# Five of sixteen row-tile pairs of the MLP's second product by Strassen's form: seven block products instead of eight

## Chip, cores and metric

One core of one Trainium2 chip runs the whole kernel as one launch. The metric is the device time of an execution in microseconds. Before the change it is 1999.34 us, the median of 3 runs (1997.73 to 1999.47).

The engines are called as in the profile: PE multiplies matrices (PEld loads its stationary operand), DVE is VectorE, ACT is ScalarE, POOL is GpSimd, SP issues most of the DMAs. Results of PE land in PSUM, which has eight accumulator banks of 128 x 512 float32.

## What is computed

The input is 256 tokens of width 2048. Two layers follow, the first with a convolution module as its mixer, the second with latent attention (MLA). After each mixer stands a squared-ReLU MLP of width 8192, all in float32:

```python
def sq_relu_mlp(h, w1, w2):
    return jnp.square(jax.nn.relu(h @ w1)) @ w2
...
    for layer in range(DEPTH):
        ...
        h = rms_norm(x, norm_mlp_g[layer])
        x = x + sq_relu_mlp(h, mlp_w1[layer], mlp_w2[layer])
    return rms_norm(x, final_norm_g)
```

The change concerns the product with `w2`, an 8192 x 2048 matrix, in both layers.

## The kernel before

**Numbers in two parts.** Each float32 operand of a product is split into a rounded part `hi` and the remainder `lo`, both of type float32r. A product is then three matmuls into the same bank: hi·hi, lo·hi, hi·lo (`mm3`, L182 to L186). Weights are loaded in units of 1 MB (`load`, L143, three `raw` buffers, issued by SP), and each unit is split in two halves (`split_half`, L152): ACT copies `raw` to `hi` (L158), DVE subtracts `hi` from `raw` (L159). `hi` and `lo` have six buffers each (`WB`, L42), each of 128 x 1024; a half takes one of each. So at most three units are split or being used at once.

**The MLP** (`mlp`, L383) works in two halves of the inner width (`HALVES`), each with 32 of the 64 row tiles of `w2`, and each in two stages:

- The first product runs in eight groups of four column tiles (L392). Weights are stationary, activations `xt` move: L403 multiplies by the 512 columns that hold both parts of 256 tokens, L404 by 256. After each group, L408 to L416 sum the parts, square the positive values and split them into `gh` and `gl`, one 128 x 256 block for each row tile of `w2`.
- The second product (`product_A`, L343) runs over four column blocks `n` of 512 columns. For each block, two PSUM banks (one for each token tile `t` of 128) collect 32 row tiles `k`: activations are stationary (`gh`, `gl`), weights of 128 x 512 move. The loop over units of four row tiles loads and splits one unit, then issues 4 x 2 x 3 matmuls. At the block's end `add` (L322, L327) adds the two banks, scaled by the token's factor `r2`, to the residual `xs`.

In the second half of each layer, finished columns of `xs` are prepared for the next stage (`prepare`, L332): transposed on PE (`to_T`, L235, L240) into PSUM banks of the kind `tr` and split into `xt`, and squared and summed on ACT (L339). One column block is prepared while the next is multiplied. In the last layer nothing is transposed; the final norm (`finish`, L1348) works on the token tiles one after the other, each after its last matmuls: the last column block holds back three units and multiplies them for `t` = 0, then for `t` = 1, so that the end of `t` = 0 lies beside the matmuls of `t` = 1. `before` (L1376) multiplies the first three column blocks by the gain ahead of that.

**PSUM.** From the convolution's second product on, the eight banks are split into six of kind `acc` and two of kind `tr` (L760).

**Order.** Outside of blocks marked `manual_schedule` (most of the two mixers) a scheduler sets each engine's order when the kernel is built: of the instructions that are ready by its own reckoning it takes the earliest in the program. Each engine then works through its list strictly in that order on the chip. A buffer is given to a new tile when its old tile has been read for the last time. The MLP lies outside of the marked blocks.

Of the kernel before, what the change touches and what calls it, by code (L numbers as in the profile page):

```python
# [10 lines left out]
F32 = mybir.dt.float32  # L11
F32R = mybir.dt.float32r
# [3 lines left out]
ALU = mybir.AluOpType  # L16
# [60 lines left out]
def trunk_kernel(  # L77
# [66 lines left out]

# [172 lines left out]
    def residual_stage(last, gain, r_scale=None):  # L317


        ssq = small.tile([P, T, NNB], F32, tag="ssq", name=nm("ssq")) if last else None  # L320

        def add(n, ps, t):  # L322
            sl = slice(n * NB, (n + 1) * NB)
            if r_scale is None:
                nc.vector.tensor_tensor(xs[:, t, sl], ps[t], xs[:, t, sl], op=ALU.add)
            else:
                nc.vector.scalar_tensor_tensor(  # L327
                    out=xs[:, t, sl], in0=ps[t], scalar=r_scale[:, t : t + 1], in1=xs[:, t, sl],
                    op0=ALU.mult, op1=ALU.add,
                )  # L330
# [49 lines left out]
        while due:  # L380
            prepare(due.pop(0))

    def mlp(layer, ssq, next_gain, finish=None, before=None):  # L383

        with ExitStack() as cx:
            mp = cx.enter_context(tc.tile_pool(name=f"mp{layer}", bufs=1, reuse_waits="tile"))
            nkh = FF // P // HALVES
            r2 = small.tile([P, T], F32, tag="r2", name=nm("r2"))
            nssq = None
            for hf in range(HALVES):  # L390
                hh, hl = [], []
                for g in range(nkh // 4):  # L392
                    ps = [acc_tile() for _ in range(4)]
                    c0 = (hf * nkh + 4 * g) * P
                    for u in range(KC // 4):
                        wj = load_split([rows(mlp_w1[layer], 4 * u, 4, c0, NB)], 4)
                        for j in range(4):
                            k = 4 * u + j
                            wh, wl = wj(j)
                            for b in range(4):  # L400
                                bs = slice(b * P, (b + 1) * P)

                                nc.tensor.matmul(ps[b], wh[:, bs], xhl(k), start=k == 0, stop=False)  # L403
                                nc.tensor.matmul(ps[b][:, :S], wl[:, bs], xh(k), start=False, stop=k == KC - 1)  # L404
                    gh = mp.tile([P, 4, S], F32R, tag="gh", name=nm("gh"), bufs=nkh // 4)
                    gl = mp.tile([P, 4, S], F32R, tag="gl", name=nm("gl"), bufs=nkh // 4)
                    for b2 in range(2):
                        v = mp.tile([P, 2, S], F32, tag="v", name=nm("v"), bufs=2)  # L408
# [4 lines left out]
                        nc.vector.scalar_tensor_tensor(out=v, in0=v, scalar=0.0, in1=v, op0=ALU.max, op1=ALU.mult)  # L413
                        bs = slice(2 * b2, 2 * b2 + 2)
                        nc.scalar.activation(gh[:, bs, :], v, AF.Copy)
                        nc.vector.tensor_tensor(gl[:, bs, :], v, gh[:, bs, :].bitcast(F32), op=ALU.subtract)  # L416
                    hh.append(gh)
                    hl.append(gl)
# [3 lines left out]
                nssq, add, prepare = residual_stage(hf == HALVES - 1, next_gain, r2)  # L422
                product_A(
                    mlp_w2[layer],
                    hf * nkh,
                    nkh,
                    lambda k, t: hh[k // 4][:, k % 4, t * P : (t + 1) * P],
                    lambda k, t: hl[k // 4][:, k % 4, t * P : (t + 1) * P],
                    add,
                    prepare,  # L430
                    finish=(lambda t: finish(nssq, t)) if finish is not None and hf == HALVES - 1 else None,
                    before=lambda: before(nssq),
                )
            return nssq


    with ExitStack() as cx:
# [218 lines left out]
        with tc.manual_schedule():  # L656
# [680 lines left out]
        product_A(mla_w_o[0], 0, H, oh_kt, ol_kt, add, prepare, range(2, NNB), range(2))  # L1337


    with tc.tile_pool(name="fin", bufs=1, reuse_waits="tile") as fp:  # L1340
        gf = fp.tile([P, D], F32, name="gf")
        nc.scalar.dma_start(gf, final_norm_g.rearrange("(a n) -> a n", a=1).partition_broadcast(P))

        def gained(t, n):
            sl = slice(n * NB, (n + 1) * NB)
            nc.vector.tensor_tensor(xs[:, t, sl], xs[:, t, sl], gf[:, sl], op=ALU.mult)

        def finish(ssq, t):  # L1348

            n = NNB - 1  # L1350
            sl = slice(n * NB, (n + 1) * NB)
            v = small.tile([P, 1], F32, tag="msf", name=nm("ms"))
            w = small.tile([P, 1], F32, tag="wsf", name=nm("ws"))
            y = small.tile([P, 1], F32, tag="ysf", name=nm("ys"))
            q = small.tile([P, 1], F32, tag="qsf", name=nm("qs"))
            nc.vector.tensor_scalar(v, ssq[:, t, n : n + 1], scalar1=1.0 / D, scalar2=part[t], op0=ALU.mult, op1=ALU.add)
            nc.scalar.activation(w, v, AF.Sqrt)
            nc.vector.reciprocal(y, w)
            nc.vector.scalar_tensor_tensor(out=q, in0=y, scalar=v, in1=y, op0=ALU.mult, op1=ALU.mult)
            nc.vector.tensor_scalar(q, q, scalar1=-0.5, scalar2=1.5, op0=ALU.mult, op1=ALU.add)  # L1360
            nc.vector.tensor_tensor(y, y, q, op=ALU.mult)
            for n in range(NNB):
                ob = xs[:, t, n * NB : (n + 1) * NB]
                if n == NNB - 1:
                    nc.vector.scalar_tensor_tensor(
                        out=ob, in0=ob, scalar=y, in1=gf[:, n * NB : (n + 1) * NB], op0=ALU.mult, op1=ALU.mult
                    )
                elif n:
                    nc.scalar.activation(ob, ob, AF.Copy, scale=y)
                else:  # L1370
                    nc.vector.tensor_scalar(ob, ob, scalar1=y, scalar2=None, op0=ALU.mult)
                nc.sync.dma_start(out[0, t * P : (t + 1) * P, n * NB : (n + 1) * NB], ob)

        part = []

        def before(ssq):  # L1376

            for t in range(T):
                m = small.tile([P, 1], F32, tag="msp", name=nm("msp"))
                nc.vector.tensor_reduce(m, ssq[:, t, : NNB - 1], axis=AX.X, op=ALU.add)  # L1380
                nc.vector.tensor_scalar(m, m, scalar1=1.0 / D, scalar2=EPS, op0=ALU.mult, op1=ALU.add)
                part.append(m)
                for n in range(NNB - 1):
                    gained(t, n)

        mlp(1, ssq, None, finish, before)


_INS = [
# [23 lines left out]
```

## Time and profile before

| | |
|---|---|
| median of 3 runs | 1999.34 us |
| profiled execution, first to last instruction (span) | 1996.1 us |
| median of the runs minus this span | 3.2 us |
| PE busy | 1971.3 us (99%) |
| DVE busy | 1212.9 us (61%) |
| ACT busy | 975.3 us (49%) |
| POOL busy | 223.8 us (11%) |
| first MLP product, first half of layer 0 | 316.4 to 494.9 us |
| second MLP product, first half of layer 0 | 494.9 to 669.0 us |

The profile is one execution, with times from the first instruction. The span leaves out what lies before the first and after the last instruction; the runs' times hold it. A matmul's row gives its duration from its start to its modelled end, and the next matmul starts before that end, so the time that a matmul costs is read from the distance between starts.

### The profile page before, as it was taken

What the parts mean: (1) busy time and instruction counts of PE and PEld (TensorE: products, weight loads), DVE (VectorE), ACT (ScalarE), POOL (GpSimd) and SP (SyncE); (2) the same over time, 40 slices, a digit from 0 to 9 for tenths busy, and PEclk for the clock granted to TensorE, in tenths of its full rate; (3) what the DMA queues carried; (4) which work ended last, traced back from release to release, by engine and by line L of the source; (5) the groups of instructions that cost most, each with busy time, mean ns of one, the idle gap of its engine ahead of it and who ended that gap; (6) DMA issues with size and microseconds to landing.
All of it is one profiled execution on the core that took longest, in us unless ns stands there. A gap on an engine that the chain in (4) does not pass through costs nothing.

```text
span 1996.1 us, 27859 instructions
## 1 busy us (share of the span) xinstructions
PE 1971.3 (99%) x11060; PEld 1728.7 (87%) x11060; DVE 1212.9 (61%) x1795; ACT 975.3 (49%) x1385; POOL 223.8 (11%) x184
## 2 busy tenths in 40 slices
PE   7999999999999999999999999999999999999998
PEld 7999888888888888888899998888888888888886
DVE  5999867556544555655556665656654545665553
ACT  5456655445333444544456665545443334454443
POOL 5999200000000000000001310000000000000000
PEclk9999999999999999999999999999999999999999
DMA  7666365665655666655555445666555566665553
GB/s 239 185 182 184 131 197 182 190 190 189 196 197 195 190 190 190 190 190 190 190 159 176 120 148 181 199 190 190 190 190 191 195 195 189 190 191 195 194 190 105
DMA packets 243265, 367.57 MB, mean 184 GB/s; under 512 B 15416, under 2 KB 89792, under 8 KB 242880
## 3 DMA queue, kind: packets, MB, share of 16 engines
q1 hardware_dynamic: 242112, 363.63, 57.8%
q10 hardware_dynamic: 1024, 2.17, 0.3%
q8 instruction: 86, 1.41, 0.3%
q14 instruction: 43, 0.35, 0.0%
HBM read 363.68 MB, written 2.10 MB: 183 GB/s over the span
## 4 chain that ended last, share of the span: by engine, by line
PE 90%; DVE 8%; ACT 1%; DMA 0%; issue 0%; POOL 0%; SPq 0%; ACTq 0%; DVEq 0%
PE acc L403 23%; PE acc L184 16%; PE acc L186 16%; PE acc L185 16%; PE acc L404 12%; DVE sum L591 6%; PE acc L490 1%; PE acc L489 1%; PE acc L491 1%; PE tr L240 1%; PE sum L539 0%; DMA xs<-in_x 0%; PE acc L1187 0%; ACT hi L158 0%; PE acc L1051 0%
## 5 line engine op out<-in xcount | busy, mean ns | idle before, releaser
L159 DVE TENSOR_TENSOR lo<-raw,hi 128x1024 fp32r<-128x1024 f32 (+2 forms) x630 | 760.7, 1210 | 694.3 <-ACT hi L158 682.6
L158 ACT ACTIVATE hi<-raw 128x1024 fp32r<-128x1024 f32 (+1 forms) x696 | 723.2, 1046 | 786.4 <-PE acc L185 450.3
L403 PE MATMUL acc<-xt,hi 128*128 128x512 f32 x2048 | 710.6, 390 | 0.0
L404 PE MATMUL acc<-xt,lo 128*128 128x256 f32 x2048 | 577.7, 282 | 0.0
L403 PEld LDWEIGHTS acc<-xt,hi 128*128 128x128 f32 x2048 | 384.5, 188 | 80.5
L184 PE MATMUL acc<-hi,gh 128*128 128x512 f32 x1024 | 398.6, 389 | 0.0
L186 PE MATMUL acc<-lo,gh 128*128 128x512 f32 x1024 | 398.4, 389 | 0.0
L185 PE MATMUL acc<-hi,gl 128*128 128x512 f32 x1024 | 398.4, 389 | 0.0
L404 PEld LDWEIGHTS acc<-xt,lo 128*128 128x128 f32 x2048 | 387.1, 189 | 0.1
L186 PEld LDWEIGHTS acc<-lo,gh 128*128 128x128 f32 x1024 | 192.2, 188 | 40.3
L184 PEld LDWEIGHTS acc<-hi,gh 128*128 128x128 f32 x1024 | 192.2, 188 | 39.6
L185 PEld LDWEIGHTS acc<-hi,gl 128*128 128x128 f32 x1024 | 192.2, 188 | 39.5
L591 DVE SCALAR_TENSOR_TENSOR sum<-ub,w_dw,sum 128x256 f32<-128x256 f32 x400 | 162.9, 484 | 7.1 <-ACT sum L547 6.0
L159 POOL TENSOR_TENSOR lo<-raw,hi 128x1024 fp32r<-128x1024 f32 x66 | 157.6, 2410 | 24.0 <-ACT hi L158 24.0
L489 PE MATMUL acc<-xt,hi 128*128 128x256 f32 x512 | 144.4, 282 | 0.0
L491 PE MATMUL acc<-xt,lo 128*128 128x256 f32 x512 | 143.1, 279 | 0.3 <-POOL lo L159 0.3
L490 PE MATMUL acc<-xt,hi 128*128 128x256 f32 x512 | 143.1, 279 | 0.1
L491 PEld LDWEIGHTS acc<-xt,lo 128*128 128x128 f32 x512 | 96.2, 188 | 0.5 <-POOL lo L159 0.5
L490 PEld LDWEIGHTS acc<-xt,hi 128*128 128x128 f32 x512 | 96.3, 188 | 0.3 <-DVE xt L197 0.3
L489 PEld LDWEIGHTS acc<-xt,hi 128*128 128x128 f32 x512 | 96.3, 188 | 0.0
L982 POOL MEMSET pad_kv<- 128x8 f32 x1 | 0.1, 104 | 770.0 <-PE acc L186 770.0
L411 ACT ACTIVATE v<-acc 128x256 f32<-128x256 f32 x128 | 46.4, 382 | 25.4 <-PE acc L404 25.4
(241 smaller groups left out, 1783.6 us busy)
## 6 DMA issues: line engine op xcount, KB each, us to landing
raw<-in_mlp_w SPq DMA_DIRECT2D x256, 1024.0 KB, 5.2
raw<-in_conv_w_pw SPq DMA_DIRECT2D x64, 512.0 KB, 5.2
raw<-in_conv_w_pw SPq DMA_DIRECT2D x16, 1024.0 KB, 5.1
raw<-in_mla_w_o SPq DMA_DIRECT2D x16, 1024.0 KB, 5.4
raw<-in_mla_w_kv_up SPq DMA_DIRECT2D x8, 1024.0 KB, 5.9
raw<-in_mla_w_in SPq DMA_DIRECT2D x8, 576.0 KB, 3.8
raw<-in_mla_w_in SPq DMA_DIRECT2D x4, 1024.0 KB, 5.4
raw<-in_mla_w_q_up SPq DMA_DIRECT2D x16, 256.0 KB, 3.8
```

Source lines behind the costliest of these rows:

```text
L158: nc.scalar.activation(hi, raw[:, js, :], AF.Copy)
L159: eng.tensor_tensor(lo, raw[:, js, :], hi.bitcast(F32), op=ALU.subtract)
L184: nc.tensor.matmul(ps, sh, mh, start=start, stop=False)
L185: nc.tensor.matmul(ps, sl, mh, start=False, stop=False)
L186: nc.tensor.matmul(ps, sh, ml, start=False, stop=stop)
L403: nc.tensor.matmul(ps[b], wh[:, bs], xhl(k), start=k == 0, stop=False)
L404: nc.tensor.matmul(ps[b][:, :S], wl[:, bs], xh(k), start=False, stop=k == KC - 1)
L411: nc.scalar.activation(v[:, b, :], o[:, S:], AF.Copy)
L489: nc.tensor.matmul(o, wh[:, bs], xh(k), start=k == 0, stop=False)
L490: nc.tensor.matmul(o, wh[:, bs], xl(k), start=False, stop=False)
L491: nc.tensor.matmul(o, wl[:, bs], xh(k), start=False, stop=k == KC - 1)
L591: nc.vector.scalar_tensor_tensor(out=out, in0=ubs[c][:, w : w + S], scalar=tap(c, w), in1=pcs[c], op0=ALU.mult, op1=ALU.add)
```

## The change

The 32 row tiles of a half become 16 pairs, and the four column blocks become two pairs `na`, `nb`. The unit of weights is now two row tiles by 1024 columns instead of four by 512, still 1 MB. For one such unit, two token tiles, two row tiles and two column blocks make a product of 2 x 2 blocks by 2 x 2 blocks. A plain pair does it in eight block products, as before. The pairs 0, 3, 6, 9 and 12 (`seven`) do it in seven, in Winograd's variant of Strassen's form: the activations' blocks are combined beforehand into seven operands (POOL, at the end of the first product), the weights' blocks are summed on DVE into four tiles `tt` before they are split, and the products are collected in seven banks, `P1`, `Q5`, `Q7`, `Q6`, `P4`, `P2`, `Q3`. With `Q0`, which takes the plain products that have no other bank, all eight are in use. After pair 12 the four banks P1, Q5, Q6 and Q7 are combined and added to `xs` (`early`), and become free. The other four take the plain products of three of the four output blocks (`outs`) beside their own, and are added at the end.

All eight banks are now of kind `acc`, and transposes take theirs from the same eight. `prepare` runs behind pairs 13 and 14 of the second pair of columns for the first two column blocks, and at the end for the other two. The last column pair of the last layer holds back pairs 13 to 15 and multiplies them by token tile; two column blocks instead of one are left for `finish`. The final gain is loaded at the start of the last second product instead of ahead of the MLP.

```diff
+        psum.clear()
...
     def tr_tile():
-        return psum["tr"].tile([P, NB], F32, tag="tr", name=nm("tr"))
+        return psum["tr"].tile([P, NB], F32, tag="tr", name=nm("tr")) if "tr" in psum else acc_tile()
...
+    def split_part(src, eng):
+        _, nj, cols = src.shape
+        hi = wpool.tile([P, nj, cols], F32R, tag="hi", name=nm("hi"), bufs=WB)
+        lo = wpool.tile([P, nj, cols], F32R, tag="lo", name=nm("lo"), bufs=WB)
+        nc.scalar.activation(hi, src, AF.Copy)
+        eng.tensor_tensor(lo, src, hi.bitcast(F32), op=ALU.subtract)
+        return hi, lo
+
+    NPAIR = FF // P // HALVES // 2
+    seven = lambda p: p % 3 == 0 and p < NPAIR - 1
+    LAST_SEVEN = max(p for p in range(NPAIR) if seven(p))
+    A11, A22, A12, S3, S1, S2, S4 = range(7)
+
+    def down(w, k_lo, hs, xs_add, prepare, pre, mp, finish=None, before=None):
+        for n2 in range(NNB // 2):
+            na, nb = 2 * n2, 2 * n2 + 1
+            banks, seen = {}, set()
+            outs = {(1, nb): "P2", (1, na): "Q3", (0, nb): "P4", (0, na): "Q0"}
+            def mm(name, sh, sl, mh, ml, stop):
+                if name not in banks:
+                    banks[name] = acc_tile()
+                mm3(banks[name], sh, sl, mh, ml, name not in seen, stop)
+                seen.add(name)
+            def plain(p, parts, n, t):
+                for k in range(2):
+                    wh, wl = parts[k]
+                    gh, gl = (a[:, k, t * P : (t + 1) * P] for a in hs[p])
+                    bs = slice((n - na) * NB, (n - na + 1) * NB)
+                    mm(outs[t, n], gh, gl, wh[:, 0, bs], wl[:, 0, bs], p == NPAIR - 1 and k == 1)
+            def early():
+                s1, s5 = (mp.tile([P, NB], F32, tag="v", name=nm("v"), bufs=2) for _ in range(2))
+                uv = mp.tile([P, 2, NB], F32, tag="W", name=nm("W"), bufs=1)
+                u, v = uv[:, 0, :], uv[:, 1, :]
+                nc.scalar.activation(s1, banks["P1"], AF.Copy)
+                nc.scalar.activation(s5, banks["Q5"], AF.Copy)
+                nc.vector.tensor_tensor(u, s1, banks["Q6"], op=ALU.subtract)
+                nc.vector.tensor_tensor(v, u, banks["Q7"], op=ALU.subtract)
+                xs_add(nb, s1, 1)
+                xs_add(nb, v, 0)
+                nc.gpsimd.tensor_tensor(u, s5, u, op=ALU.subtract)
+                nc.gpsimd.tensor_tensor(v, s5, v, op=ALU.subtract)
+                xs_add(na, u, 1)
+                xs_add(na, v, 0)
+            last = finish is not None and n2 == NNB // 2 - 1
+            kept = []
+            for p in range(NPAIR):
+                raw = load([rows(w, k_lo + 2 * p, 2, na * NB, 2 * NB)], 2)
+                if seven(p):
+                    x = raw.rearrange("p j (b n) -> p (j b) n", b=2)
+                    tt = mp.tile([P, 4, NB], F32, tag="T", name=nm("T"), bufs=1)
+                    nc.vector.tensor_tensor(
+                        tt[:, 0:2, :], x[:, 0:1, :].broadcast_to([P, 2, NB]), x[:, 1:3, :], op=ALU.add
+                    )
+                    one = split_part(x[:, 1:2, :], nc.vector)
+                    nc.vector.tensor_tensor(tt[:, 2, :], tt[:, 0, :], x[:, 2, :], op=ALU.add)
+                    t13 = split_part(tt[:, 0:2, :], nc.vector)
+                    nc.vector.tensor_tensor(tt[:, 3, :], tt[:, 2, :], x[:, 3, :], op=ALU.add)
+                    t24 = split_part(tt[:, 2:4, :], nc.vector)
+                    two = split_part(x[:, 2:4, :], nc.vector)
+                    gh, gl = hs[p]
+                    for name, f, part, i in (
+                        ("P1", A11, one, 0), ("Q5", S1, t13, 0), ("Q7", S3, t13, 1), ("Q6", S2, t24, 0),
+                        ("P4", A22, t24, 1), ("P2", A12, two, 1), ("Q3", S4, two, 0),
+                    ):
+                        mm(name, gh[:, f, :], gl[:, f, :], part[0][:, i, :], part[1][:, i, :],
+                           p == LAST_SEVEN and name in ("P1", "Q5", "Q6", "Q7"))
+                    if p == LAST_SEVEN:
+                        early()
+                else:
+                    parts = [split_half(raw, h, nc.vector) for h in range(2)]
+                    if last and p > LAST_SEVEN:
+                        kept.append((p, parts))
+                    else:
+                        for t in range(T):
+                            for n in (na, nb):
+                                plain(p, parts, n, t)
+                    if p > LAST_SEVEN and pre:
+                        prepare(pre.pop(0))
+            if last:
+                before()
+                for t in range(T):
+                    for n in (nb, na):
+                        for p, parts in kept:
+                            plain(p, parts, n, t)
+                        xs_add(n, banks[outs[t, n]], t)
+                        prepare(n, t)
+                    finish(t)
+            else:
+                for t, n in ((0, nb), (1, nb), (1, na), (0, na)):
+                    xs_add(n, banks[outs[t, n]], t)
+                pre += [na, nb]
...
+                        if seven(p):
+                            f = mp.tile([P, 8, P], F32, tag="W", name=nm("W"), bufs=1)
...
+                            nc.gpsimd.tensor_tensor(
+                                f[:, 4:6, :], f[:, 0:1, :].broadcast_to([P, 2, P]), f[:, 1:3, :], op=ALU.subtract
+                            )
+                            nc.gpsimd.tensor_tensor(f[:, 6, :], f[:, 1, :], f[:, 5, :], op=ALU.subtract)
+                            nc.gpsimd.tensor_tensor(f[:, 7, :], f[:, 3, :], f[:, 6, :], op=ALU.subtract)
+                            src, shape, tag = f[:, 1:8, :], [P, 7, P], "s"
...
+                        nc.scalar.activation(gh, src, AF.Copy)
+                        nc.vector.tensor_tensor(gl, src, gh.bitcast(F32), op=ALU.subtract)
+                        hs.append((gh, gl))
...
-            repool("m", acc=6, tr=2)
+            repool("m", acc=8)
...
         for n in range(NNB):
             ob = xs[:, t, n * NB : (n + 1) * NB]
-            if n == NNB - 1:
+            if n >= NNB // 2:
                 nc.vector.scalar_tensor_tensor(
...
                 )
-            elif n:
-                nc.scalar.activation(ob, ob, AF.Copy, scale=y)
             else:
-                nc.vector.tensor_scalar(ob, ob, scalar1=y, scalar2=None, op0=ALU.mult)
+                nc.scalar.activation(ob, ob, AF.Copy, scale=y)
```

More of the change, by code (lines that the diff above doesn't have):

```diff
@@ L381, in product_A @@
             prepare(due.pop(0))
-    def mlp(layer, ssq, next_gain, finish=None, before=None):
+    def split_part(src, eng):
[7 more added lines that the diff above has]
+    seven = lambda p: p % 3 == 0 and p < NPAIR - 1
@@ new lines, in trunk_kernel @@
+    LAST_SEVEN = max(p for p in range(NPAIR) if seven(p))
[78 more added lines that the diff above has]
+                pre += [na, nb]
+        if finish is None:
+            while pre:
+                prepare(pre.pop(0))
@@ L385, in mlp @@
+    def mlp(layer, ssq, next_gain, finish=None, before=None, last_w1=None):
         with ExitStack() as cx:
@@ L404, in mlp @@
                                 nc.tensor.matmul(ps[b][:, :S], wl[:, bs], xh(k), start=False, stop=k == KC - 1)
-                    gh = mp.tile([P, 4, S], F32R, tag="gh", name=nm("gh"), bufs=nkh // 4)
-                    gl = mp.tile([P, 4, S], F32R, tag="gl", name=nm("gl"), bufs=nkh // 4)
                     for b2 in range(2):
+                        p = 2 * g + b2
                         v = mp.tile([P, 2, S], F32, tag="v", name=nm("v"), bufs=2)
@@ L421, in mlp, with xs_add @@
                     nc.vector.tensor_tensor(r2, r, r, op=ALU.mult)
[L422 to L430, printed above, removed]
+                if hf == HALVES - 1 and last_w1 is not None:
+                    last_w1()
+                nssq, _, prepare = residual_stage(hf == HALVES - 1, next_gain, r2)
+                def xs_add(n, src, t):
+                    sl = slice(n * NB, (n + 1) * NB)
+                    nc.vector.scalar_tensor_tensor(
+                        out=xs[:, t, sl], in0=src, scalar=r2[:, t : t + 1], in1=xs[:, t, sl], op0=ALU.mult, op1=ALU.add
+                    )
+                down(
+                    mlp_w2[layer], hf * nkh, hs, xs_add, prepare if hf == HALVES - 1 else lambda *a: None, [], mp,
                     finish=(lambda t: finish(nssq, t)) if finish is not None and hf == HALVES - 1 else None,
@@ L1337, in trunk_kernel, with load_gain @@
         product_A(mla_w_o[0], 0, H, oh_kt, ol_kt, add, prepare, range(2, NNB), range(2))
-    with tc.tile_pool(name="fin", bufs=1, reuse_waits="tile") as fp:
-        gf = fp.tile([P, D], F32, name="gf")
+    fin = {}
+    def load_gain():
+        fp = right_pool("fin", 1)
+        fin["g"] = gf = fp.tile([P, D], F32, name="gf")
         nc.scalar.dma_start(gf, final_norm_g.rearrange("(a n) -> a n", a=1).partition_broadcast(P))
[L1344 to L1363, printed above, removed]
-                if n == NNB - 1:
-                    nc.vector.scalar_tensor_tensor(
-                        out=ob, in0=ob, scalar=y, in1=gf[:, n * NB : (n + 1) * NB], op0=ALU.mult, op1=ALU.mult
-                    )
-                elif n:
-                    nc.scalar.activation(ob, ob, AF.Copy, scale=y)
[L1370 to L1386, printed above, removed]
@@ L1389, with before @@
+    part = []
+    def before(ssq):
+        for t in range(T):
+            m = small.tile([P, 1], F32, tag="msp", name=nm("msp"))
+            nc.vector.tensor_reduce(m, ssq[:, t, : NNB // 2], axis=AX.X, op=ALU.add)
+            nc.vector.tensor_scalar(m, m, scalar1=1.0 / D, scalar2=EPS, op0=ALU.mult, op1=ALU.add)
+            part.append(m)
+            for n in range(NNB // 2):
+                gained(t, n)
+    mlp(1, ssq, None, finish, before, load_gain)
 _INS = [
```

46 lines of the change are left out of this document (39 added, 7 removed).

## The prediction

> **What bounds the kernel now.** I read the page's busy line, its clock row and its chain first, then PE's waits.
>
> ```profile
> span 1996.1 us, 27859 instructions
> ...
> PE 1971.3 (99%) x11060; PEld 1728.7 (87%) x11060; DVE 1212.9 (61%) x1795; ACT 975.3 (49%) x1385; POOL 223.8 (11%) x184
> ...
> PEclk9999999999999999999999999999999999999999
> ...
> PE 90%; DVE 8%; ACT 1%; DMA 0%; issue 0%; POOL 0%; SPq 0%; ACTq 0%; DVEq 0%
> ```
>
> ```profile
> PE tr L280 <- DMA stage<-in_conv_w_dw: 11.7, 1, 11.7
> PE sum L539 <- DVE ub L514: 2.1, 1, 2.1
> PE tr L1178 <- DVE pr L1172: 1.2, 2, 0.9
> ```
>
> PE is busy for 99% of the span at full clock, the chain that ends last is PE's for 90%, and the three longest waits of PE stand at the start, in the convolution and in the MLA; none is in the MLP. So a matmul taken out of the MLP shortens the span by what it costs PE, as long as nothing else becomes late. What it costs is not the duration of its row. Below are a group by shape, and the first and last rows of the timeline of PE over the second product of layer 0's first half (columns: start, duration, engine, line).
>
> ```profile
> L184 PE MATMUL acc<-hi,gh 128*128 128x512 f32 x1024 | 398.6, 389 | 0.0
> ```
>
> ```profile
> 494.91 0.39 PE L184 MATMUL acc<-hi,gh 128*128 128x512 f32 x1
> 495.14 0.40 PE L185 MATMUL acc<-hi,gl 128*128 128x512 f32 x1
> ...
> 668.78 0.39 PE L186 MATMUL acc<-lo,gh 128*128 128x512 f32 x1
> 669.01 0.40 PE L403 MATMUL acc<-xt,hi 128*128 128x512 f32 x1
> ```
>
> 32 row tiles x 4 blocks x 2 token tiles x 3 matmuls are 768 starts in 669.01 - 494.91 = 174.10 us: **226.7 ns** apart, while each row lasts 389 ns, since a matmul starts before the last one's modelled end. I take 226.7 ns.
>
> **What the change removes.** A seven-pair issues 7 x 3 = 21 matmuls where eight products take 24. There are 5 such pairs x 2 column pairs x 2 halves x 2 layers = 40, so 120 matmuls go: 120 x 0.2267 = **27.2 us**. A plain pair takes PE 24 x 0.2267 = 5.44 us, a seven-pair 4.76 us.
>
> The Trainium skill ("TensorE: Matmul & The Clock Gate", Back-to-back issue gap) gives a warm gap of N/2.4 + 2.5 ns, an estimate of 215.8 ns for N = 512 and of 25.9 us for the change. The trace's 226.7 ns is longer and decides.
>
> **What it adds on DVE, ACT and POOL.** The durations come from the groups by shape:
>
> ```profile
> L159 DVE TENSOR_TENSOR lo<-raw,hi 128x1024 fp32r<-128x1024 f32 x606 | 742.4, 1228 | 675.9 <-ACT hi L158 664.3 <-PE tr L240 9.6
> L158 ACT ACTIVATE hi<-raw 128x1024 fp32r<-128x1024 f32 x672 | 707.3, 1060 | 769.9 <-PE acc L185 433.7 <-PE acc L403 301.7 <-ACT gh L415 27.2
> L159 POOL TENSOR_TENSOR lo<-raw,hi 128x1024 fp32r<-128x1024 f32 x66 | 157.6, 2410 | 24.0 <-ACT hi L158 24.0
> ...
> L416 DVE TENSOR_TENSOR gl<-v,gh 128x512 fp32r<-128x512 f32 x64 | 43.8, 684 | 0.0
> L415 ACT ACTIVATE gh<-v 128x512 fp32r<-128x512 f32 x64 | 40.5, 633 | 6.3 <-DVE v L413 6.3
> ...
> L327 DVE SCALAR_TENSOR_TENSOR xs<-acc,r,xs 128x512 f32<-128x512 f32 x32 | 23.0, 751 | 11.0 <-PE acc L186 11.0
> ...
> L567 POOL TENSOR_TENSOR tp<-tp,tp 128x256 f32<-128x256 f32 x23 | 16.9, 742 | 0.2
> ...
> L325 DVE TENSOR_TENSOR xs<-acc,xs 128x512 f32<-128x512 f32 x16 | 10.6, 687 | 3.0 <-PE acc L186 3.0
> ...
> L1269 ACT ACTIVATE cq<-acc,y 128x512 f32<-128x512 f32 x2 | 1.4, 690 | 0.5 <-PE acc L186 0.5
> ```
>
> *A seven-pair.* DVE: the four sums (1.23 + 2 x 0.68 = 2.60 us), the split of `one` (0.68) and of three tiles of 1024 columns (3 x 1.23): 6.96 us, against 2.46 for a plain pair. ACT: 0.63 + 3 x 1.06 = 3.81 us against 2.12. So DVE needs more time for a seven-pair (6.96) than PE (4.76). Over three pairs, seven and plain and plain, it is 6.96 + 2 x 2.46 = 11.9 us beside PE's 4.76 + 2 x 5.44 = 15.64 us, 76%. The load fits; whether it comes in time hangs on the buffers.
>
> *`early`*, 8 times: on ACT two copies from PSUM (2 x 0.69), on DVE two differences (2 x 0.69) and four additions to `xs` (4 x 0.75), 4.4 us; on POOL two differences of 512 columns, half of 2.41 us each, 1.2 us (estimate). The four additions at the end of a column pair are as many as before.
>
> *Operands of the seven*, 20 times, on POOL: one operation of 256 columns (0.74 us) and two of 128. These lie in the first product, and pairs 0 to 12 are not multiplied until that is over.
>
> POOL and DVE hold each other up. Rows of both timelines in the MLA:
>
> ```profile
> 1108.16 0.47 POOL L898 TENSOR_TENSOR m<-scratch,cos 128x128 f32<-128x128 f32 x1
> 1108.58 1.45 POOL L899 TENSOR_TENSOR m<-scratch,sin 128x128 f32<-128x128 f32 x1
> ```
>
> ```profile
> 1108.16 1.55 DVE L159 TENSOR_TENSOR lo<-raw,hi 128x1024 fp32r<-128x1024 f32 x1 [2.20 <-ACT hi L158]
> ```
>
> The same POOL operation lasts 0.47 or 1.45 us, the second beside a DVE split, which itself lasts 1.55 instead of 1.23. So I allow the longer of the two for each POOL step on a chain: `early` takes 4.4 + 2 x 1.2 + 2 waits of about 0.75, some 8 us from its first step.
>
> In all DVE gains 40 x 4.5 + 8 x 4.4 + some 8 for wider operand splits, about 223 us (to 1436, 73% of the span), ACT about 85.
>
> **Do the weights come in time?** Today ACT waits for a buffer, not for data:
>
> ```profile
> 503.11 1.06 ACT L158 ACTIVATE hi<-raw 128x1024 fp32r<-128x1024 f32 x1 [1.65 <-PE acc L185]
> ```
>
> ```profile
> raw<-in_mlp_w SPq DMA_DIRECT2D x256, 1024.0 KB, 5.2
> ```
>
> The idle time ahead of a split ends when PE gives `hi` back; a load lands 5.2 us after its issue. I follow the six `hi`/`lo` buffers through three pairs, counted from a seven-pair's first matmul. It frees its four tiles after 3, 9, 15 and 21 matmuls: 0.68, 2.04, 3.40, 4.76 us. The plain pairs free theirs at 9.52, 10.20 and 14.96, 15.64. Each new tile takes the buffer of the tile six before it. The next seven-pair's tiles get theirs at 3.40, 4.76, 9.52 and 10.20; with 1.06 of ACT and 1.23 of DVE, and a neighbour queued ahead, its last is ready by about 13.7 and is needed at 15.64 + 15 x 0.2267 = 19.04. Its other tiles have 5 us or more. The plain pair after it gets buffers at 14.96 and 15.64, is ready by about 18.5 and is needed at 20.40. The last plain pair has 5 us. Loads: the `raw` of a seven-pair is free at about 13, lands 5.2 us later and isn't split before 19. So no step of the cycle is late; the margin is 2 to 5 us.
>
> **Seams**, where the margin is thinner:
>
> *First to second product* (4 times). In the same place today DVE does the sums of the last group and then the split of the last buffer to come free:
>
> ```profile
> 498.94 1.22 DVE L159 TENSOR_TENSOR lo<-raw,hi 128x1024 fp32r<-128x1024 f32 x1
> ```
>
> It ends 5.25 us after the second product's first matmul (494.91). In the changed kernel that is the `lo` of pair 1's second half, needed after 4.76 + 5 x 0.2267 = 5.9 us. A margin of 0.65 us; I take a loss of 0.2 each, 0 to 1.
>
> *Column pair to column pair* (4 times, and 4 ends of a half). Four banks are free since `early`; P4's is needed after 12 matmuls, 2.72 us, the others 0.68 us apart, and four additions of 0.75 us free them at that pace from 0.75 us on. Cover: 2 us, unless DVE puts two splits ahead. I take 0.15 each, 0 to 3.
>
> *End of layer 0.* 16 transposes instead of 8 follow the last matmul and wait for four additions. Today such transposes lie among the next stage's matmuls:
>
> ```profile
> 1024.32 0.30 PE L186 MATMUL acc<-lo,xt 128*128 128x288 f32 x1
> 1024.46 0.82 PE L240 MATMUL tr<-ident,xs 128*128 128x128 f32 x6
> 1025.03 0.38 PE L184 MATMUL acc<-hi,xt 128*128 128x288 f32 x1
> ```
>
> The MLA's first row tiles are ready by then, so they can go first: 0 to 3 us, I take 0.3.
>
> *The end.* Pairs 13 to 15 are held back and are read within 18 matmuls. Pair 15 gets the last buffers of pair 12 at its end, and `early` and `before` (4 x 0.68 us) compete for DVE: 0 to 3 us, I take 1. Behind the last matmul:
>
> ```profile
> 1987.29 0.75 DVE L327 SCALAR_TENSOR_TENSOR xs<-acc,r,xs 128x512 f32<-128x512 f32 x1 [4.14 <-PE acc L186]
> ...
> 1990.20 0.48 DVE L1371 TENSOR_SCALAR xs<-xs,ys 128x512 f32<-128x512 f32 x1
> 1990.61 0.74 DVE L1365 SCALAR_TENSOR_TENSOR xs<-xs,ys,gf 128x512 f32<-128x512 f32 x1
> ```
>
> DVE scales two blocks by the longer form, 0.27 us more. The gain's 1 MB load moves beside the second product, where loads wait for buffers anyway: nothing, or one load of 5.2 us late.
>
> The losses sum to 4 x 0.2 + 4 x 0.15 + 0.3 + 1 + 0.3 = 3.0 us. The sum is -27.2 + 3.0 = **-24.2 us**: a span of 1971.9 from 1996.1, and as the median of the runs lies 3.2 us above the span, **1975.1 us** from 1999.34.
>
> **Rivals.**
>
> *No bank to change to.* With all eight banks collecting, PE stands while four sums leave PSUM. If four additions (3.0 us) lay on the path at each of the 8 ends, 24 of the 27.2 us would be lost: about 1996; with half of them, 1984. For it: DVE is the busier engine, and a split ahead of an addition costs 1.23 us. Against it: `early` empties four banks ahead of the end. The Trainium skill ("Perfetto Trace Analysis", Matmuls) says that independent groups should rotate through banks, so that the evacuation of one lies beside the matmuls of the next. This change leaves only `early`'s four for that; no row of before shows all eight in use.
>
> *DVE in the wrong order* (slower). Each engine's list is fixed at build time. If a sum of the next seven-pair, waiting for its load, stands ahead of splits that PE needs, look-ahead is lost there, and PE waits for what DVE needs over PE's time (6.96 - 4.76 = 2.2 us) and for the first `hi` and `lo` (1.3 us), 3.5 us. It decides from 27.2 / 3.5 = 8 of the 40 seven-pairs. At 16 it gives 2028, at all 40 some 2112. For it: only six buffers, four to a seven-pair. Against it: the margins above, and that today's order keeps PE without a wait in the MLP.
>
> *No change*: both in part, 1995.3 to 2003.3. *More than forecast*: if a matmul cost its 389 ns, 46.7 us would go, 1953; the 768 starts speak against it. That the change doesn't remove its matmuls is excluded by the count.
>
> **How the numbers follow.** Forecast (1970 to 1979) 0.58; the banks or a few late splits take part of the gain (1979 to 1995.3) 0.20; no change 0.05; slower 0.14 (2003 to 2050 mostly); more 0.03. A measurement of this kernel can tell about 0.2%, 4 us, from no change: faster 0.81, same 0.05, slower 0.14. A range of 1970 to 1998 takes in the first two cases and part of the third, about 0.8.
>
> **What would show it.** Right: L184 to L186 have 120 fewer matmuls of 512 columns on the MLP's tiles, with starts 0.227 us apart; a second product of one half takes (768 - 30) x 0.2267 = 167.3 us instead of 174.1; DVE about 1436 us. Wrong: a wait of PE for `hi` or `lo` in each seven-pair (order), or for `xs` (banks); or starts that lie further apart.

## The result and the profile after

The changed kernel takes **1974.44 us** (median of 4 runs, 1974.37 to 1974.63), beside 1998.61 for the kernel before in the same measurements. The ratio is 0.988, with a 95% interval of 0.987 to 0.990. The forecast was 1975.1 us, with a loss of 3.0 against the 27.2 us of the removed matmuls. The measured loss is about as large, and lies at another place. Single executions of the kernel before lie near 1997.8 or near 1999.4 us, so its median depends on how many of each were taken. The profiled executions, 1996.1 and 1972.6 us from the first to the last instruction, differ by 23.5 us, a loss of 3.7.

The page of the changed kernel: span, busy times, and the clock by slices.

```profile
span 1972.6 us, 28263 instructions
...
PE 1945.4 (99%) x10940; PEld 1708.3 (87%) x10940; DVE 1410.4 (71%) x2043; ACT 1032.7 (52%) x1481; POOL 311.0 (16%) x260
...
PEclk9999999999999999999999999999999999999999
```

PE has 120 matmuls fewer, and is still busy for 99%. DVE was busy for 197.5 us more, where 223 were forecast. PE's waits:

```profile
PE tr L281 <- DMA stage<-in_conv_b_dw: 11.6, 1, 11.6
PE sum L669 <- DVE ub L644: 2.1, 1, 2.1
PE acc L187 <- DVE lo L160: 2.0, 1, 2.0
PE acc L1308 <- DVE pr L1302: 1.0, 1, 1.0
```

One line of the MLP is new: a single wait of 2.0 us for a `lo` (counted from the modelled end of the matmul ahead of it; by the distance of starts below it is 2.2). The ends of the other column pairs, all seven-pairs and all four seams from the first to the second product are without a wait of PE that is listed. The first second product, by the starts of its first matmul and of the first one after it:

```profile
494.36 0.39 PE L185 MATMUL acc<-hi,sh 128*128 128x512 f32 x1
...
661.65 0.40 PE L514 MATMUL acc<-xt,hi 128*128 128x512 f32 x1
```

661.65 - 494.36 = 167.29 us; the prediction worked out 167.3 for 738 matmuls 226.7 ns apart. The same readings give 167.3 us for the first half of layer 1. From the first matmul of layer 0's second half to that of the next first product (the MLA lies between) it is 430.0 us instead of 436.4, 0.4 short of the full 6.8. The last second product, from its first start (1792.21) to its last (1963.22, below), takes 171.0 us where 167.1 would be full speed. These 3.9 us are about the whole loss.

The timeline of PE there (the first line is the first start of this product), then DVE and POOL at the end of it:

```profile
1792.21 0.39 PE L185 MATMUL acc<-hi,sh 128*128 128x512 f32 x1
...
1948.17 0.39 PE L187 MATMUL acc<-lo,gh 128*128 128x512 f32 x1
1948.40 0.39 PE L185 MATMUL acc<-hi,gh 128*128 128x512 f32 x1
1950.82 0.50 PE L187 MATMUL acc<-lo,gh 128*128 128x512 f32 x1 [2.04 <-DVE lo L160]
...
1953.73 0.63 PE L187 MATMUL acc<-lo,gh 128*128 128x512 f32 x1
1954.16 0.63 PE L185 MATMUL acc<-hi,gh 128*128 128x512 f32 x1
...
1963.22 0.39 PE L187 MATMUL acc<-lo,gh 128*128 128x512 f32 x1
```

```profile
1944.12 1.22 DVE L160 TENSOR_TENSOR lo<-raw,hi 128x1024 fp32r<-128x1024 f32 x1
1945.26 2.44 DVE L555 SCALAR_TENSOR_TENSOR xs<-W,r,xs 128x512 f32<-128x512 f32 x2
1948.88 0.75 DVE L555 SCALAR_TENSOR_TENSOR xs<-W,r,xs 128x512 f32<-128x512 f32 x1 [1.18 <-POOL W L438]
1949.55 2.35 DVE L160 TENSOR_TENSOR lo<-raw,hi 128x1024 fp32r<-128x1024 f32 x2
```

```profile
1944.35 2.13 POOL L437 TENSOR_TENSOR W<-v,W 128x512 f32<-128x512 f32 x1 [79.13 <-DVE W L434]
1947.12 1.73 POOL L438 TENSOR_TENSOR W<-v,W 128x512 f32<-128x512 f32 x1 [0.63 <-DVE xs L555]
```

In the last column pair of the last layer the `lo` of pair 15 (1949.55) stands in DVE's list behind the fourth addition of `early`, which waits 1.18 us for POOL. From the start at 1948.40 to the next at 1950.82 it is 2.42 us instead of 0.227, a wait of 2.2 us. From about 1951.4 on, matmuls start 0.427 us apart for some 3.6 us: about half speed. The table of windows of the same kernel (columns: window, its length, busy time and instructions of PE, PEld, DVE, ACT and POOL, granted clock with 1.00 as full speed, DMA share, GB/s) says that the granted clock was lower there:

```profile
1943.00:1948.00 5.00, 5.00 (x24) 4.14 (x23) 4.70 (x5) 1.53 (x2) 3.02 (x2) 1.00 0.00 0
1948.00:1951.00 3.00, 0.96 (x5) 0.50 (x4) 2.12 (x3) 0.00 (x0) 0.85 (x1) 1.00 0.00 0
1951.00:1956.00 5.00, 5.00 (x16) 3.92 (x17) 2.19 (x3) 0.72 (x2) 0.00 (x0) 0.66 0.00 0
```

A granted clock of 0.66 over 5 us costs (1 - 0.66) x 5 = 1.7 us. With the wait of 2.2 us it makes up the 3.9.

### The profile page after: what moved, and what is told of

It is laid out like the page before. It is cut to its first block, busy times and chain, and to the rows that moved or that the text cites. A ratio compares the mean times of both kernels' runs of the same rounds, so it can differ in the third digit from the quotient of the medians.

```text
span 1972.6 us, 28263 instructions
## 1 busy us (share of the span) xinstructions
PE 1945.4 (99%) x10940; PEld 1708.3 (87%) x10940; DVE 1410.4 (71%) x2043; ACT 1032.7 (52%) x1481; POOL 311.0 (16%) x260
## 3 DMA queue, kind: packets, MB, share of 16 engines
q10 hardware_dynamic: 1024, 2.17, 0.3%
q8 instruction: 85, 1.39, 0.3%
## 4 chain that ended last, share of the span: by engine, by line
PE 89%; DVE 8%; ACT 1%; DMA 1%; issue 0%; POOL 0%; POOLq 0%; DVEq 0%; ACTq 0%
PE acc L514 24%; PE acc L187 15%; PE acc L186 15%; PE acc L185 15%; PE acc L515 12%; DVE sum L721 6%; PE acc L620 1%; PE acc L621 1%; PE acc L619 1%; PE acc L241 1%; DVE lo L160 1%; PE sum L669 0%; ACT hi L159 0%; PE acc L1317 0%; DMA xs<-in_x 0%
## 5 line engine op out<-in xcount | busy, mean ns | idle before, releaser
L160 DVE TENSOR_TENSOR lo<-raw,hi 128x1024 fp32r<-128x1024 f32 (+1 forms) x550 | 651.4, 1207 | 367.7 <-ACT hi L159 360.9
L159 ACT ACTIVATE hi<-raw 128x1024 fp32r<-128x1024 f32 (+2 forms) x616 | 622.5, 1040 | 432.4 <-PE acc L514 227.4
L514 PEld LDWEIGHTS acc<-xt,hi 128*128 128x128 f32 x2048 | 384.4, 188 | 79.7
L515 PEld LDWEIGHTS acc<-xt,lo 128*128 128x128 f32 x2048 | 388.0, 189 | 0.1
L187 PE MATMUL acc<-lo,gh 128*128 128x512 f32 x704 | 274.9, 391 | 2.0 <-DVE lo L160 2.0
L185 PE MATMUL acc<-hi,gh 128*128 128x512 f32 x704 | 274.8, 390 | 0.0
L186 PE MATMUL acc<-hi,gl 128*128 128x512 f32 x704 | 274.7, 390 | 0.0
L185 PE MATMUL acc<-hi,sh 128*128 128x512 f32 x408 | 159.6, 391 | 0.0
L187 PE MATMUL acc<-lo,sh 128*128 128x512 f32 x408 | 159.0, 390 | 0.0
L185 PEld LDWEIGHTS acc<-hi,gh 128*128 128x128 f32 x704 | 132.5, 188 | 27.2
L390 DVE TENSOR_TENSOR lo<-T,hi 128x1024 fp32r<-128x1024 f32 x80 | 97.9, 1225 | 51.6 <-ACT hi L389 51.3
```

The lines of the kernel that those rows point to most:

```text
L159: nc.scalar.activation(hi, raw[:, js, :], AF.Copy)
L160: eng.tensor_tensor(lo, raw[:, js, :], hi.bitcast(F32), op=ALU.subtract)
L185: nc.tensor.matmul(ps, sh, mh, start=start, stop=False)
L186: nc.tensor.matmul(ps, sl, mh, start=False, stop=False)
L187: nc.tensor.matmul(ps, sh, ml, start=False, stop=stop)
L390: eng.tensor_tensor(lo, src, hi.bitcast(F32), op=ALU.subtract)
```

## Experiments

Two theories were tested against rivals: that the gain is the removed matmuls at 226.7 ns and nothing else; and that the weights come in time because of some 5 us of look-ahead (the time by which a split is ready ahead of the matmul that needs it), with the one loss at the end being a matter of DVE's order. The experiments ran later than the changed kernel, beside the kernel before, whose median was then 1997.8 us. All kernels do the whole computation; they differ in order, in an engine or in which pairs are seven-pairs.

### No seven-pair

```diff
-    seven = lambda p: p % 3 == 0 and p < NPAIR - 1
-    LAST_SEVEN = max(p for p in range(NPAIR) if seven(p))
+    seven = lambda p: False
+    LAST_SEVEN = 12
```

> No pair by the seven products: all sixteen pairs plain, everything else of the change kept (units of two row tiles by 1024 columns, eight banks of one kind, the order at the end). No early combination is left. Theory (the gain is the 120 matmuls at 0.2267 us each, and the rearrangement alone is worth nothing): 1974.4 + 27.2 - 3.9 for the wait and slow stretch at the end, which go with early: 1997.7 (1996.5 to 1999.5), a second product of one half 174.1 us long again. Rival (part of the gain is from the new units, banks or order): 1985 to 1995.

Measured: 1997.7 us, beside 1997.8 for the kernel before (ratio 0.9999, 0.999 to 1.0008). Its timeline of PE over the first second product:

```profile
494.40 0.39 PE L185 MATMUL acc<-hi,gh 128*128 128x512 f32 x1
...
668.49 0.40 PE L514 MATMUL acc<-xt,hi 128*128 128x512 f32 x1
```

174.09 us for 768 matmuls, as before the change. So the new units, the eight banks of one kind and the new end are by themselves worth nothing that can be told from no change (0.1%), and the gain comes with the removed matmuls.

### The late early combination

```diff
-                    if p == LAST_SEVEN:
+                    if p == LAST_SEVEN and not last:
                         early()
...
             if last:
+                early()
                 before()
```

> In the last column pair of the last layer alone, the combination of the four early banks stands behind the splits of the held-back pairs in the program. In the changed kernel's trace PE stands once in the MLP, from 1948.40 to 1950.82 us, until DVE has made the lo of pair 15, and from 1951.4 to 1955.1 nine matmuls start 0.427 instead of 0.227 us apart at a granted clock of 0.66. Theory (order on DVE: the last early addition, which waits for POOL, stands ahead of that lo, and the slow stretch follows from PE's wait): both go, 2.2 + 1.8 us, about 1970.4 us (1970.0 to 1971.5), with the clock at 1.0 throughout. Rival (DVE has too much to do there in any order, or hi comes late): the wait stays, 1973.5 to 1974.5. Second rival (the slow stretch has a cause of its own): only the wait goes, 1972.2 with the slow stretch still there.

Measured: 1970.46 us (ratio to before 0.986, 0.985 to 0.988), 4.0 us less than the changed kernel, as by the spans (1968.6 against 1972.6). DVE now makes five of the six splits of the held-back pairs in one run, and the sixth behind the first difference of the combination; PE doesn't wait there, the product takes 167.1 us, and the clock stays up. The timeline of DVE and the same windows as above:

```profile
1938.84 5.77 DVE L160 TENSOR_TENSOR lo<-raw,hi 128x1024 fp32r<-128x1024 f32 x5 [3.08 <-ACT hi L159]
1944.53 0.68 DVE L433 TENSOR_TENSOR W<-v,acc 128x512 f32<-128x512 f32 x1
1945.12 1.22 DVE L160 TENSOR_TENSOR lo<-raw,hi 128x1024 fp32r<-128x1024 f32 x1
```

```profile
1943.00:1948.00 5.00, 5.00 (x24) 4.14 (x23) 5.00 (x7) 1.51 (x3) 0.92 (x1) 1.00 0.00 0
1948.00:1951.00 3.00, 3.00 (x15) 2.50 (x14) 1.96 (x2) 0.00 (x0) 2.37 (x2) 1.00 0.00 0
1951.00:1956.00 5.00, 5.00 (x24) 4.14 (x23) 2.88 (x8) 1.65 (x5) 0.10 (x1) 1.00 0.00 0
```

The wait and the slow stretch went together, as the theory has it. DVE's work is the same, so its amount was not the cause; its order was. The run doesn't say whether a wait of another length would have been followed by the lower clock; the run with five in a row, below, says something of that.

### The early differences on DVE

```diff
-                nc.gpsimd.tensor_tensor(u, s5, u, op=ALU.subtract)
-                nc.gpsimd.tensor_tensor(v, s5, v, op=ALU.subtract)
+                nc.vector.tensor_tensor(u, s5, u, op=ALU.subtract)
+                nc.vector.tensor_tensor(v, s5, v, op=ALU.subtract)
```

> The two differences that POOL makes in the combination of the early banks (2.12 and 1.74 us there, beside DVE) are made by DVE instead (0.68 us each), everywhere. Theory (order on DVE): DVE is then without its 1.2 us wait for POOL, but has 1.2 us more to do ahead of the lo of pair 15, so PE's wait of 2.2 us at the end stays within 0.6 us: 1973.5 to 1974.8. Rival (POOL holding up DVE is the cause of that wait): the wait is gone and the clock stays up, about 1970.4. No other column pair changes in either case, since there PE doesn't wait.

Measured: 1970.50 us. My expectation failed; the time is the rival's. The timeline of DVE from the addition ahead of the differences to the `lo` of pair 15:

```profile
1945.22 0.74 DVE L555 SCALAR_TENSOR_TENSOR xs<-W,r,xs 128x512 f32<-128x512 f32 x1
1945.89 0.68 DVE L437 TENSOR_TENSOR W<-v,W 128x512 f32<-128x512 f32 x1
1946.49 0.68 DVE L438 TENSOR_TENSOR W<-v,W 128x512 f32<-128x512 f32 x1
1947.09 1.41 DVE L555 SCALAR_TENSOR_TENSOR xs<-W,r,xs 128x512 f32<-128x512 f32 x2
1948.42 2.35 DVE L160 TENSOR_TENSOR lo<-raw,hi 128x1024 fp32r<-128x1024 f32 x2
```

The `lo` starts 1.1 us earlier (1948.42 against 1949.55), though DVE does more: it has no 1.18 us of waiting for POOL, and two additions that had taken 2.44 us beside POOL take 1.41. I had counted them at twice 0.75. The rest is not POOL's. In this build PE has five other matmuls, 1.1 us of work, between the place where it stood before and the first that needs this `lo`. So the run changed two things. It says that POOL's part is about half of the wait: with PE's order as it was, this `lo`, which ends near 1949.6, would still have come about 1.0 us late (an estimate, against 1948.40 + 0.227).

### Five seven-pairs in a row

```diff
-    seven = lambda p: p % 3 == 0 and p < NPAIR - 1
+    seven = lambda p: 8 <= p <= 12
```

> Still five pairs by the seven products, but in a row: 8, 9, 10, 11, 12 instead of 0, 3, 6, 9, 12. The matmuls are as many. Theory (a seven-pair needs 6.5 us of DVE in a row, from the trace of the changed kernel, beside 4.76 of PE, and is paid for by the plain pairs around it; look-ahead is worth some 5 us): in each of the eight column pairs DVE falls behind by 4 x 1.8 = 7.2 us and 5 us of look-ahead cover part, so 2 us lost (0 to 7): 1990 us (1975 to 2030), with PE waiting for lo in pairs 11 to 13. Rival (the place of the seven-pairs doesn't matter, since DVE is 71% busy on the whole): 1974.4. Second rival (any seven-pair without plain pairs ahead loses all its 3.5 us): 1974.4 + 4 x 8 x 3.5 = 2086.

Measured: 2035.02 us (2032.72 to 2038.13; ratio 1.018, 1.017 to 1.020): slower than before the change, with as many matmuls as the changed kernel, and outside the 1975 to 2030 that I gave. Its waits of PE, and its timeline of DVE over one seven-pair within the row:

```profile
PE acc L185 <- ACT hi L389: 15.2, 16, 1.5
PE acc L187 <- DVE lo L160: 12.8, 8, 1.9
...
PE acc L187 <- DVE lo L390: 8.2, 16, 0.6
```

```profile
542.31 1.22 DVE L449 TENSOR_TENSOR T<-raw 128x1024 f32<-128x1024 f32 x1
543.45 0.68 DVE L390 TENSOR_TENSOR lo<-raw,hi 128x512 fp32r<-128x512 f32 x1
544.05 0.68 DVE L453 TENSOR_TENSOR T<-T,raw 128x512 f32<-128x512 f32 x1
544.74 1.23 DVE L390 TENSOR_TENSOR lo<-T,hi 128x1024 fp32r<-128x1024 f32 x1
545.88 0.68 DVE L455 TENSOR_TENSOR T<-T,raw 128x512 f32<-128x512 f32 x1
547.77 1.22 DVE L390 TENSOR_TENSOR lo<-T,hi 128x1024 fp32r<-128x1024 f32 x1 [1.21 <-ACT hi L389]
548.92 1.22 DVE L390 TENSOR_TENSOR lo<-raw,hi 128x1024 fp32r<-128x1024 f32 x1
550.05 1.22 DVE L449 TENSOR_TENSOR T<-raw 128x1024 f32<-128x1024 f32 x1
```

From one seven-pair's first sum to the next it is 550.05 - 542.31 = 7.74 us, not the 6.5 that I took: after the last sum DVE has nothing to do until ACT has made that sum's `hi`. Against PE's 4.76 us, four steps lose 11.9 us. The first second product takes 182.15 us (494.25 to 676.40), 14.9 more than in the changed kernel. By column pair it is 90.8 and 91.35 us where 369 matmuls at full speed take 83.65: 7.2 and 7.7 us lost. In the second, matmuls start 0.43 us apart from about 655 to 658.7 us, and the granted clock over 650 to 660 us is 0.83, some 1.7 us of the 7.7. So look-ahead covers about 4.8 of the 11.9 us in the first column pair and 5.9 in the second, near the 5 that I took; the step that I had too small was DVE's 6.5 us. The place of the seven-pairs decides between 1974 and 2035 us; the mean load of DVE (70% here) shows nothing of it.

The run also has five waits of PE for the `lo` of a plain pair, each 2.28 to 2.30 us from start to start. Behind three of them (starts at 934.58, 1917.64 and 2010.10 us) matmuls start 0.43 us apart for about 3.4 us; behind the other two (574.92 and 1557.94) they go on 0.23 us apart. Two of the windows:

```profile
574.00:580.00 6.00, 5.08 (x22) 4.17 (x23) 6.00 (x6) 2.06 (x3) 0.00 (x0) 1.00 0.50 144
934.00:940.00 6.00, 5.42 (x17) 4.30 (x18) 6.00 (x6) 2.01 (x2) 0.00 (x0) 0.72 0.53 154
```

So waits of one length have either outcome, and what decides between them is not shown. The run has five slow stretches that cost about 1.7 us each (an estimate from the granted clock of such windows), the changed kernel has one; so some 7 of the 58 us by which this profile is longer go with the clock.

### Every second pair, and more of them

With the late combination, five pairs (4, 6, 8, 10, 12), then six (0, 2, 5, 7, 10, 12), then seven (0, 2, ... 12). For the last two, two of the weight sums are written over blocks of the loaded tile, which frees memory for the additional operands.

```diff
-    seven = lambda p: p % 3 == 0 and p < NPAIR - 1
+    seven = lambda p: p in (4, 6, 8, 10, 12)
```

> Five pairs by the seven products again, now every second one (4, 6, 8, 10, 12), with the late early combination of e1_early_late. From the run with five in a row: a seven-pair takes 7.7 us of DVE when nothing else is ready, since its last sum, ACT's hi of it and DVE's lo of it follow one another; a plain pair 2.3. Theory (DVE's time over a stretch, less some 5 us of look-ahead, against PE's 4.76 + 5.44 = 10.2): 7.7 + 2.3 = 10.0 fits just, nothing lost, 1970.5 us (1970 to 1973). Rival (a seven-pair needs two plain pairs behind it, or look-ahead drains): 0.5 to 1.5 us lost in each of 4 x 8 places, 1986 to 2010.

```diff
-                    tt = mp.tile([P, 4, NB], F32, tag="T", name=nm("T"), bufs=1)
+                    tt = mp.tile([P, 2, NB], F32, tag="T", name=nm("T"), bufs=1)
...
-                    nc.vector.tensor_tensor(tt[:, 2, :], tt[:, 0, :], x[:, 2, :], op=ALU.add)
+                    nc.vector.tensor_tensor(x[:, 0, :], tt[:, 0, :], x[:, 2, :], op=ALU.add)
...
-                    nc.vector.tensor_tensor(tt[:, 3, :], tt[:, 2, :], x[:, 3, :], op=ALU.add)
-                    t24 = split_part(tt[:, 2:4, :], nc.vector)
+                    nc.vector.tensor_tensor(x[:, 1, :], x[:, 0, :], x[:, 3, :], op=ALU.add)
+                    t24 = split_part(x[:, 0:2, :], nc.vector)
```

> Six pairs by the seven products (0, 2, 5, 7, 10, 12), with the late early combination; two of the four weight sums are written over blocks of the loaded tile that are read by then, which frees 4 KB for the sixth pair's operands. Theory: 8 x 3 = 24 matmuls less than e1_early_late, 5.4 us: 1965.0 us (1964 to 1968), a second product of one half (768 - 36) x 0.2267 = 165.9 us. Rival (the sums over the loaded tile hold its buffer or DVE longer, or DVE is at its end): 1970 or above.

```diff
-                        v = mp.tile([P, 2, S], F32, tag="v", name=nm("v"), bufs=2)
+                        v = mp.tile([P, 2, S], F32, tag="v", name=nm("v"), bufs=1)
...
-                s1, s5 = (mp.tile([P, NB], F32, tag="v", name=nm("v"), bufs=2) for _ in range(2))
+                s15 = mp.tile([P, 2, NB], F32, tag="T", name=nm("T"), bufs=1)
+                s1, s5 = s15[:, 0, :], s15[:, 1, :]
```

> Seven pairs by the seven products (0, 2, 4, 6, 8, 10, 12), as e9_six, with one buffer instead of two for the sums at the end of a group of the first product, and the two copies of the early combination in the place of the weight sums. Theory: 48 matmuls less than e1_early_late, 10.9 us: 1959.6 us (1958.5 to 1964), if DVE's 10.0 of 10.2 us holds over 13 pairs. Rival (DVE is the bound there: any further work, such as the additions at a column pair's end, is paid for in full): 2.9 to 7.3 us lost in each of 8 column pairs, 1983 to 2018.

Measured: five 1970.80 us, six 1969.75 (1968.36 to 1970.33), seven 1967.70 (ratio to before 0.985, 0.984 to 0.986). With five, every second pair loses nothing, so one plain pair behind each is enough. Beyond five, the gains over the late combination are 0.7 and 2.8 us instead of 5.4 and 10.9, both outside the ranges that I gave. With six, PE waits at the beginning of each second column pair, and DVE's timeline shows for what:

```profile
577.12 1.23 DVE L449 TENSOR_TENSOR T<-raw 128x1024 f32<-128x1024 f32 x1 [1.61 <-DMA raw<-in_mlp_w]
...
578.93 1.22 DVE L390 TENSOR_TENSOR lo<-raw,hi 128x1024 fp32r<-128x1024 f32 x1
...
580.72 1.22 DVE L390 TENSOR_TENSOR lo<-raw,hi 128x1024 fp32r<-128x1024 f32 x1
581.85 1.41 DVE L556 SCALAR_TENSOR_TENSOR xs<-acc,r,xs 128x512 f32<-128x512 f32 x2
583.17 2.36 DVE L160 TENSOR_TENSOR lo<-raw,hi 128x1024 fp32r<-128x1024 f32 x2
```

A sum of the next seven-pair but one waits 1.61 us for its load, ahead of splits of pairs 0 and 1 (578.93 to 583.17) that could have gone first; PE then waits 0.3 us for each half of pair 1. That is the wrong order that the slower rival described, at a small price. The first second product takes 166.8 us instead of 165.9: its first column pair runs at full speed (82.97 us for 366 matmuls), and the second loses the 0.9. The other three lose as much each (0.90 to 0.95), 3.7 us in all; the list of waits shows 1.2 of it, since it counts from the modelled end of the matmul ahead. The two profiled executions are 0.1 us apart, and the rest of what is missing from 5.4 us lies outside of the change: the one with six is already 1.7 us behind the late combination when the first MLP product begins (317.72 against 316.06), ahead of all code that differs.

Seven lose in the same way at the beginning of each second column pair, and also at the end of the kernel: the last second product takes 167.7 us where 164.4 would be full speed, with two waits for `lo` near 1941 and 1943 us. With the other three (1.4, 1.0 and 1.8 us) it is 7.5 of the 10.9 us.

## Why the prediction was right

*The matmul's price.* Right and shown: 738 matmuls took 167.29 us against 167.3 forecast, and without seven-pairs the time of before is back within 0.1%. The rows' 389 ns would have given 46.7 us.

*The gap between matmuls.* The first of the two second products of each layer takes 6.8 us less than before, 30 x 0.227 us, so the measured spacing decides. The Trainium skill ("TensorE: Matmul & The Clock Gate", Back-to-back issue gap) gives N/2.4 + 2.5 ns for an isolated matmul, an estimate of 25.9 us for the 120; for a stream of weight loads and matmuls it gives about 131 ns at N = 512, an estimate of 15.7 us. The trace's 226.7 ns agrees with neither.

*Look-ahead.* Right, and shown by the row. The prediction had the next seven-pair's last tile ready 13.7 us after a seven-pair's start and the plain pair's behind it at 18.5. In layer 1's first half, pair 6 starts at 1478.70, and these two end at 1491.7 and 1497.1, 13.0 and 18.4 us later. ACT starts on the latter 15.0 us after the start, when the prediction has its buffer come free (14.96); the row doesn't name what ended ACT's idle time:

```profile
1490.47 1.22 DVE L390 TENSOR_TENSOR lo<-raw,hi 128x1024 fp32r<-128x1024 f32 x1
1494.77 4.63 DVE L160 TENSOR_TENSOR lo<-raw,hi 128x1024 fp32r<-128x1024 f32 x4 [3.08 <-ACT hi L159]
```

```profile
1493.68 3.90 ACT L159 ACTIVATE hi<-raw 128x1024 fp32r<-128x1024 f32 x4 [3.43 <-issue]
```

DVE's time for a seven-pair was taken too short where nothing lies between (6.96 us of instructions, 7.74 in a row): the wait of 1.21 us for ACT inside it was left out. With plain pairs between, the wait is still there (1.39 us in pair 9 here), but DVE has time for it.

*Seams.* 0.8 us from the first to the second product and 0.6 at the column pairs' ends were forecast; no wait is there. The rival "no bank to change to" is out: the seven ends of column pairs that have more work of PE behind them pass without a listed wait for a bank, with four banks emptied ahead. The end of layer 0 cost at most the 0.4 us that its half is short of the full gain, where 0.3 was forecast. The Trainium skill ("Perfetto Trace Analysis", Matmuls) wants independent groups to rotate through the banks, so that emptying one lies beside the matmuls of the next. The trace agrees in so far as four of eight banks were enough for that.

*The end.* The mechanism was right (pair 15 against `early` on DVE, 0 to 3 us, taken at 1), the size was not: 2.2 us of wait, and 1.7 us by the clock, which the prediction left out. The price of POOL's steps was too low: 1.2 us each by half of a longer row, 2.12 and 1.74 us in all eight places.

*The sum.* That it is right to 0.7 us is in part luck. 1.4 us too much at the seams and 2.9 too little at the end leave 1.5. Some of that is made up by the first second product, which begins 0.55 us earlier (494.36 against 494.91) before any seven-pair has run. So the span of 1971.9 us that was forecast is 0.7 too low. The forecast of the runs' median is 0.7 too high instead, since it added 3.2 us to the span: it set a median of 1999.34 against one profiled execution, while each execution of the record takes 1.8 us more than its own span (1974.39 and 1972.6, for one).

*Slower by DVE's order.* It didn't happen at this spacing. The run with six shows this order, at 0.9 us for each place and not 3.5. The run with five in a row shows another way to lose the look-ahead, too much of DVE's work in one stretch: 60 us more with as many matmuls.

## What to carry to other kernels

Take the price of a matmul from the distance of starts in the stage, and check it by a kernel that has everything of the change but the saving. Where work moves from PE to DVE, don't compare totals: follow the few buffers through one cycle, count the waits between engines within one step, and put lighter steps behind each heavy one. Look at the last stretch by itself, where there is no later work to fill a wait and where a combination that isn't urgent can stand in the list ahead of what PE needs.

## What the runs showed of the hardware

- A wait of PE of 2.2 us in an otherwise full stretch was followed by some 3.6 us at about half speed (starts 0.427 us apart, granted clock 0.66 over 1951 to 1956 us); without the wait the clock stayed at 1.00. With five in a row, three of five waits of 2.28 to 2.30 us between starts had such a stretch behind them (granted clock 0.72 over 6 us) and two had none (1.00), so length alone doesn't decide.
- A difference of 128 x 512 on POOL took 2.13 us beside an addition of DVE, and 1.73 us where DVE stood for most of it. Two additions of DVE took 2.44 us with POOL at work, 1.41 when POOL did nothing.
- Matmuls of 128 x 512 in this form start 226.7 ns apart though each row lasts 389 ns; 120 of them taken out of a busy PE were worth 23.5 us of span, and 27.4 with the wait at the end gone (1996.0 without seven-pairs against 1968.6).
